# Q and K tiles with their heads' rows interleaved, each stored as 128 rows by one transfer

## The chip, the cores and the metric

The kernel runs on one core of a Trainium2 chip. A core has five engines with instruction streams of their own: TensorE (PE, the matmuls; PEld is its weight load), VectorE (DVE), ScalarE (ACT), GpSimd (POOL) and SyncE (SP). Here SP issues every DMA, in order. The transfers themselves run on the core's 16 DMA engines. Data lies in DRAM, in SBUF (128 partitions) or in PSUM (eight banks, which PE writes). The metric is the device time of one launch in microseconds: the median before is 1924.31 us over three runs (1919.36 to 1927.94).

## The reference, cut to what matters

Two layers over 2048 latent tokens of width 1024, with 256 context tokens. Layer 0 (even) runs windowed attention (8 query heads, 2 key/value heads of 64 dimensions, a sink for each head) beside a bidirectional S5 scan, both from one projection; layer 1 (odd) is a pooling mixer. The change touches the queries and keys of layer 0:

```python
q, k, v, g_attn, u, g_ssm = jnp.split(a @ w_in, cuts, axis=-1)
q = apply_axial_rope(q.reshape(b, l, ATTN_HEADS, HEAD_DIM), cos, sin)
k = apply_axial_rope(k.reshape(b, l, ATTN_KV_HEADS, HEAD_DIM), cos, sin)
...
s_loc = jnp.einsum('bnqhgd,bnkhd->bnhgqk', qb, kb).astype(jnp.float32) * scale
s_ctx = jnp.einsum('bnqhgd,bkhd->bnhgqk', qb, kc).astype(jnp.float32) * scale
p = jax.nn.softmax(jnp.concatenate([s_loc, s_ctx, s_sink], axis=-1), axis=-1)
out = (jnp.einsum('bnhgqk,bnkhd->bnqhgd', p_loc, vb)
       + jnp.einsum('bnhgqk,bkhd->bnqhgd', p_ctx, vc))
```

A score sums over the 64 dimensions of a head, so any order of these dimensions gives the same score if Q and K share it.

## The kernel before

Everything is fp32, and large products are made from parts: a value is split into a high part (float32r) and the rest (`split`, line 577), and a projection takes three matmuls for each block of 128 inputs (`products`, line 1020).

**The stages.** Up to about 90 us the kernel forms the adaptive-norm vectors and the statistics of the rows. Then come the projections: first those of u for the S5 scan, with K and V of the context (`t_u`), then `t_main` over two halves of the tokens. For each half it projects tiles of 128 columns by 512 tokens: m = 4 is K (both heads), m = 5 is V, m = 6 to 9 are Q (two heads each), m = 10 to 17 are gates. Between these matmuls stand those of S5: `t_s5u` loads u for a pair of channel groups from `u_scr` (line 1375), `t_s5e` tables from `e_scr`, `t_s5out` loads from `o_scr` and `r_scr` (lines 1529 and 1532) and stores the result to `z_scr` (line 1579). From about 690 us the attention runs in 32 units of one K/V head and 128 queries: `t_kv` loads and splits K and transposes V, `t_qk` loads Q and forms scores for four heads, DVE adds the mask and takes the maximum, ACT takes the exponential, POOL scales, PE transposes, and `t_pv` multiplies with V. The gates of the second half fill PE between. From about 1290 us on there is only layer 1, nearly all PE.

**A Q or K tile.** One PSUM bank holds a tile. Its 128 rows are [first rotation half of head A, the same of head B, second half of A, second half of B], 32 rows each, so the rotation is three products on DVE with cosine and sine (lines 1291 to 1293) and one sum on POOL (line 1297). The sum is stored to DRAM by two transfers (lines 1298 to 1300): rows 0 to 63 to the first 32 dimensions of two heads, rows 64 to 127 to the other 32. On the DRAM side such a transfer has the pattern [2 heads, 32 rows, 512 tokens]. K of the context goes the same way (line 1224).

**The loads.** `t_kv` needs K of one head twice, in partitions 0 to 63 and 64 to 127. It reads it by one transfer whose pattern begins with a step of zero taken twice, [0, 2], then 64 rows (line 1699); then it loads V (line 1700, 64 rows). Each job is loaded one job ahead of its use (line 1705). `t_qk` reads four heads by 128 queries into each half of the partitions, two transfers of 64 rows for each unit (lines 1765 to 1767), two units ahead.

**What sets the order.** The program's parts are generators, and a planner (`Threads`, lines 119 to 289) runs the one that is ready first by a model of costs; the order in which it runs them is the order of the instructions on each engine. For a DMA (`dma`, lines 220 to 239) the model keeps SP busy 0.55 us where either side has more than two dimensions, else 0.36 us for runs of 512 elements or more and 0.43 us for shorter ones; it holds a transfer back until the eighth one before it has landed (line 222), and it counts the data as spread over 16 engines, whatever the pattern. All DMAs are issued by line 513, all elementwise products and sums by line 465, activations by 499, matmuls by 505 and transposes by 509, so a line of the profile is told apart by its tiles: `x_r`, `core_r` and the like are regions of SBUF, `q_scr`, `k_scr`, `v_scr`, `u_scr`, `e_scr`, `o_scr`, `z_scr` and `sg_scr` (gates) are DRAM.

Of the kernel before, what the change touches and what calls it, by code (L numbers as in the profile page):

```python
# [15 lines left out]
T = 2048  # L16
D = 1024
CTX = 256
# [272 lines left out]
def body(ctx: ExitStack, tc: tile.TileContext, I, out):  # L291
# [34 lines left out]
        return drp.tile(list(shape), F32, name=name)  # L326

    a_scr = dram("a_scr", 2, KT, 128, 512)
    q_scr = dram("q_scr", 8, 64, T)
    k_scr = dram("k_scr", 2, 64, T + CTX)  # L330
    v_scr = dram("v_scr", 128, T + CTX)
    sg_scr = dram("sg_scr", 8, 128, T)
    u_scr = dram("u_scr", NG, L, 16, UCH)
# [845 lines left out]
    def t_u():  # L1179
        yield from wait("a4")  # L1180
        kv = yield from need(lambda: Ring(2, CTX))
        ub = {}
        for q in ORDER:
            yield from wait(f"a{q}")
            n = 512 if q < 4 else CTX
            tiles = range(6) if q == 4 else (0, 1, 2, 3) if q != ORDER[-1] else (2, 3, 0, 1)
            for m in tiles:
                yield from wait(f"wu{m}")
                if m < 4 and q in (4, ORDER[1]):
                    ub[q == 4, m] = yield from need(lambda: Buf(L, CCH if q == 4 else 64))  # L1190
                b = yield from gemm_bank()
                ps = bank(b, n)
                w = [shaped(wu[m].bufs[i].f, (KT, 128)) for i in range(2)]
                yield from products(ps, w, acts[q], last=m == tiles[-1] and q > 1)
                if tiles[0] == 2 and m == 3:
                    wu[2].free()
                    wu[3].free()
                k0, nk = (32 * (q % 2), 32) if q < 4 else (0, CCH)

                def evac(ps=ps, m=m, k0=k0, nk=nk, q=q, b=b):  # L1200
                    if m < 4:
                        o = ub[q == 4, m].f[:, ::-1, k0:k0 + nk].rearrange("p j k -> p k j")
                        act(o, ps.rearrange("p (k j) -> p k j", j=L), AF.Copy)
                        put_bank(b)
                        if q == 4 or q % 2 == 1:
                            def store():
                                src = ub[q == 4, m]
                                x0, nx = (0, CCH) if q == 4 else (CCH + 32 * (q - 1), 64)
                                for g in range(8):
                                    dma(u_scr[8 * m + g].rearrange("j c x -> c j x")[:, :, x0:x0 + nx],  # L1210
                                        src.f[16 * g:16 * g + 16])
                                if q in (4, ORDER[-1]):
                                    src.free()

                            todo.append(store)
                        return
                    o = kv.next()
                    act(o, ps, AF.Copy)
                    put_bank(b)

                    def store():
                        if m == 4:
                            for half in range(2):
                                dma(k_scr[:, 32 * half:32 * half + 32, T:], o[64 * half:64 * half + 64])
                        else:
                            dma(v_scr[:, T:], o)

                    todo.insert(0, store)

                todo.append(evac)  # L1230
            if q == 4:
                for r in wu[4:]:
                    r.free()
        for q in (0, 1):
            acts["b", q] = acts[q]
            flags.add(f"b{q}")
        yield from drain()
        for b in (kv, *wu[:2]):
            b.free()
        flags.add("u")  # L1240
# [9 lines left out]
    def t_main():  # L1250
        yield from t_u()
        yield from need(stage.fill)
        rope = yield from need(lambda: Ring(2, 2, 512))
        yield from wait("W0")
        W = s5.pop("W")
        yield from reopen("x1", X1, F32)
        flags.add("x1f")
        for h in range(2):
            tabs = []
            for c in range(2):  # L1260
                t_ = rope.next()
                dma(t_, I["rope"][:, :, 1024 * h + 512 * c:1024 * h + 512 * (c + 1)])
                tabs.append(t_)
            tiles = [(m + d, c) for m in range(4, 18, 2) for c in range(2) for d in range(2)]
            if h == 1:
                tiles = [x for x in tiles if x[0] < SOLO] + [(m, c) for c in range(2) for m in range(SOLO, 18)]
            for m, c in tiles:
                q = 2 * h + c
                yield from wait(f"b{q}")
                b = yield from gemm_bank()  # L1270
                ps = bank(b)
                j = 14 * h + m - 4
                alone = h == 1 and m >= SOLO
                if alone:
                    j += (18 - SOLO) * c
                if j == 10:
                    flags.add("again")
                if h == 1 and m == SOLO:
                    flags.add("kvqg_last")
                yield from products(ps, W.get(j, alone or c == 1), acts["b", q], last=m == 17)  # L1280

                def evac(ps=ps, m=m, t0=512 * q, tab=tabs[c], b=b):
                    if m == 5:
                        o = stage.next()
                        act(o, ps, AF.Copy)
                        put_bank(b)
                        todo.insert(0, lambda: dma(v_scr[:, t0:t0 + 512], o))
                    elif m < 10:
                        cos, sin = tab[:, 0], tab[:, 1]
                        t1, t2 = stage.next(), stage.next()  # L1290
                        tt(V, t1, ps, cos, OP.mult)
                        tt(V, t2[0:64], ps[64:128], sin[64:128], OP.mult)
                        tt(V, t2[64:128], ps[0:64], sin[0:64], OP.mult)
                        put_bank(b)

                        def more():
                            tt(G, t1, t1, t2, OP.add)
                            dst = k_scr if m == 4 else q_scr[2 * (m - 6):2 * (m - 6) + 2]
                            for half in range(2):
                                dma(dst[:, 32 * half:32 * half + 32, t0:t0 + 512], t1[64 * half:64 * half + 64])  # L1300
                            if (m, t0) == (9, 1536):
                                rope.free()

                        todo.insert(0, more)
                    else:
                        t1, t2 = stage.next(), stage.next()
                        act(t1, ps, AF.Tanh, scale=0.5)

                        def more():
                            stt(t2, t1, 1.0, ps, OP.add, OP.mult)  # L1310
                            put_bank(b)
                            todo.insert(0, lambda: dma(sg_scr[m - 10, :, t0:t0 + 512], t2))

                        todo.insert(0, more)

                todo.append(evac)
        W.free()
        flags.add("kvqg_w")
        yield from drain()
        flags.add("kvqg")  # L1320

        yield from t_out0()
        yield from t_l2()
        flags.add("end")
# [346 lines left out]
    def t_kv():  # L1671
# [12 lines left out]
        for s in range(8):  # L1684
            kv, n = UNITS[4 * s]
# [9 lines left out]
        def load(i):  # L1695
            if i < len(jobs):
                _, kv, _, _, t0, n, _ = jobs[i]
                r, v = raw.next()[:, :n], vt.next()[0:64, :n]
                dma(r, dap(k_scr, kv * 64 * (T + CTX) + t0, [0, 2], [T + CTX, 64], [1, n]))
                dma(v, v_scr[64 * kv:64 * kv + 64, t0:t0 + n])  # L1700
                got[i] = r, v

# [44 lines left out]
    def t_qk():  # L1747
# [13 lines left out]
        def load(u):  # L1761
            if u < NU:
                kv, n = UNITS[u]
                r = shaped(qraw.next(), (4, 128))
                for e in range(2):
                    dma(r[64 * e:64 * e + 64],
                        q_scr[4 * kv:4 * kv + 4, :, 128 * n:128 * n + 128].rearrange("h d t -> d h t"))
                qs[u] = r

        def prep(u):  # L1770
# [812 lines left out]
def _constants():  # L2583
# [30 lines left out]
    ang = np.stack([row[:, None] * inv, col[:, None] * inv], axis=1).reshape(T, 32).T  # L2614
    cos, sin = np.cos(ang).astype(f), np.sin(ang).astype(f)
    rope = np.zeros((128, 2, T), f)
    for b in range(4):
        rope[32 * b:32 * b + 32, 0] = cos
        rope[32 * b:32 * b + 32, 1] = sin if b < 2 else -sin
    return cst, rope  # L2620


def _layout(i):
# [26 lines left out]
    x1 = np.concatenate([np.arange(16), 32 + np.arange(16)])  # L2650
    x2 = x1 + 16
    order = [1280 + np.arange(512)]
    order.append(np.concatenate([512 + 64 * h + x for x in (x1, x2) for h in range(2)]))
    order.append(640 + np.arange(128))
    for p in range(4):
        order.append(np.concatenate([64 * h + x for x in (x1, x2) for h in (2 * p, 2 * p + 1)]))
    order.append(768 + np.arange(512))
    order.append(1792 + np.arange(512))
    order = np.concatenate(order)
# [47 lines left out]
```

## Time and profile before

| | |
|---|---|
| median of 3 runs | 1924.31 us |
| the profiled execution's own time | 1923.84 us |
| its span in the profile | 1921.9 us |
| mean granted TensorE clock | 0.957 |
| DMA packets, bytes | 241720, 286.16 MB |
| busy time of PE from 298 to 690 us | 367.68 of 392 us |
| busy time of PE from 690 to 1170 us | 384.04 of 480 us |

The page of a profile gives the busy time of each engine; the chain of waits goes back from the last instruction through whatever released each step, and gives start and length of each piece. A piece named DMA lasts from the issue to the landing. A piece named SPq is time of SP's queue. In a timeline the bracket after an instruction is the idle time of its engine before it, and what ended it. A row of windows gives, for each stretch, the busy time and the number of instructions of each engine, then the clock granted to TensorE, the mean busy share of the 16 DMA engines and what they moved.

### The profile page before, as it was taken

The page shows a single profiled execution, that of the slowest core. Times are in us where ns is not written, and L with a number is a line of the kernel's source. Part 1 is how long each engine was busy: PE and PEld are TensorE (multiplying, and loading weights), DVE is VectorE, ACT ScalarE, POOL GpSimd, SP SyncE. Part 2 cuts the span into 40 slices and gives each one's busy share as a digit, 9 for nine tenths or more (in the row PEclk, how much of TensorE's full clock was granted, in tenths as well). Part 3 has the DMA queues.
Part 4 walks back from the last instruction along what each step waited for, and adds up shares of the span by engine and source line. Part 5 has one row for each costly group of instructions (what it writes and reads, how often), then busy time and mean ns, then how long its engine had stood idle before and what let it go on. Part 6 is the DMA issues. An engine that isn't in the chain of part 4 may idle for free.

```text
span 1921.9 us, 24924 instructions
## 1 busy us (share of the span) xinstructions
PE 1753.0 (91%) x8488; PEld 1390.8 (72%) x8488; DVE 1284.6 (67%) x2182; ACT 827.9 (43%) x1689; POOL 549.2 (29%) x691
## 2 busy tenths in 40 slices
PE   7899998899998987878777898999899999999997
PEld 2554576678887865667666677888788888888897
DVE  4567869988886535576667875877555675566644
ACT  4545422355543424466665665644322243222321
POOL 4875653532433101242334542530000000000000
PEclk9999999999998987889898999999999999999999
DMA  8776483356654452444455563787411145351232
GB/s 294 211 251 198 130 251 117 113 158 201 191 184 128 127 171 69 109 122 124 134 160 154 151 183 93 221 266 230 129 53 55 44 154 185 115 153 61 87 94 86
DMA packets 241720, 286.16 MB, mean 149 GB/s; under 512 B 75832, under 2 KB 170808, under 8 KB 240568
## 3 DMA queue, kind: packets, MB, share of 16 engines
q1 hardware_dynamic: 241592, 284.56, 48.9%
q8 instruction: 67, 1.10, 0.2%
q14 instruction: 61, 0.50, 0.1%
HBM read 204.60 MB, written 79.89 MB: 148 GB/s over the span
## 4 chain that ended last, share of the span: by engine, by line
PE 68%; DVE 11%; DMA 8%; ACT 5%; issue 4%; POOL 3%; SPq 2%; DVEq 0%; ACTq 0%; POOLq 0%
PE psum L505 65%; PE psum L509 3%; DVE core_f L465 3%; DVE x_r L465 2%; ACT x_f L499 2%; SPq L513 2%; DVE x_f L484 2%; ACT x_r L499 1%; DMA x_f<-u_scr 1%; DVE core_f L476 1%; POOL core_f L465 1%; ACT core_f L499 1%; POOL core_f L470 1%; DVE core_r L465 1%; DMA o_scr<-core_f 1%
## 5 line engine op out<-in xcount | busy, mean ns | idle before, releaser
L505 PE MATMUL psum<-x_r,core_r 128*128 128x512 f32 (+3 forms) x4536 | 1104.1, 398 | 23.7 <-DVE x_r L465 11.0
L505 PEld LDWEIGHTS psum<-x_r,core_r 128*128 128x128 f32 x4536 | 850.2, 192 | 224.8 <-issue 22.3
L505 PE MATMUL psum<-x_r 128*128 128x256 f32 (+3 forms) x1808 | 378.9, 351 | 33.0 <-ACT core_f L499 16.1
L465 DVE TENSOR_TENSOR core_f<-core_f 128x512 f32<-128x512 f32 (+18 forms) x556 | 374.0, 694 | 49.6 <-ACT core_f L499 17.6
L505 PEld LDWEIGHTS psum<-x_r 128*128 128x128 f32 x1808 | 295.8, 198 | 76.1 <-ACT core_f L499 21.0
L465 DVE TENSOR_TENSOR core_r<-core_f,core_r 128x512 fp32r<-128x512 f32 (+1 forms) x172 | 127.7, 743 | 182.7 <-ACT core_r L499 182.6
L499 ACT ACTIVATE core_r<-core_f 128x512 fp32r<-128x512 f32 (+1 forms) x224 | 140.6, 631 | 245.2 <-PE psum L505 124.6
L465 POOL TENSOR_TENSOR core_f<-core_f 128x32 f32<-128x32 f32 (+5 forms) x257 | 164.8, 654 | 201.2 <-DVE core_f L465 61.6
L499 ACT ACTIVATE core_f<-psum 128x512 f32<-128x512 f32 (+2 forms) x217 | 115.4, 534 | 205.1 <-PE psum L505 158.2
L471 POOL TENSOR_SCALAR x_f<-x_f,core_f 128x640 f32<-128x640 f32 (+1 forms) x128 | 128.9, 1020 | 208.8 <-DVE core_f L493 164.2
L499 ACT ACTIVATE x_r<-core_f 128x512 fp32r<-128x512 f32 (+5 forms) x174 | 127.4, 744 | 110.4 <-DVE core_f L476 72.1
L484 DVE CUSTOM_DVE_ANT_0 x_f<-psum,x_f 128x640 f32<-128x640 f32 (+1 forms) x128 | 98.7, 771 | 113.3 <-PE psum L505 111.6
L499 ACT ACTIVATE x_f<-x_f,core_f 128x640 f32<-128x640 f32 (+2 forms) x154 | 122.7, 798 | 98.6 <-DVE core_f L476 94.8
L509 PE MATMUL psum<-core_f,x_f 128*128 128x128 f32 (+1 forms) x728 | 116.7, 285 | 25.0 <-DVE x_r L465 17.4
L499 ACT ACTIVATE core_f<-core_f 64x32 f32<-64x32 f32 (+8 forms) x225 | 84.1, 375 | 125.5 <-DVE core_f L476 100.5
L465 POOL TENSOR_TENSOR core_r<-core_f,core_r 128x512 fp32r<-128x512 f32 x52 | 77.3, 1489 | 204.7 <-ACT core_r L499 196.1
L476 DVE SCALAR_TENSOR_TENSOR core_f<-core_f 128x512 f32<-128x512 f32 (+13 forms) x162 | 118.2, 739 | 18.9 <-DMA core_f<-h_scr 11.6
L499 ACT ACTIVATE x_r<-psum 128x512 fp32r<-128x512 f32 (+2 forms) x174 | 96.5, 561 | 75.7 <-PE psum L505 59.5
L499 ACT ACTIVATE x_f<-psum 128x512 f32<-128x512 f32 (+5 forms) x187 | 77.5, 447 | 118.5 <-PE psum L505 104.2
L509 PEld LDWEIGHTS psum<-core_f,x_f 128*128 128x128 f32 (+1 forms) x728 | 90.9, 148 | 47.8 <-DVE x_r L465 24.0
L505 PE MATMUL psum<-x_f 128*128 128x128 f32 (+1 forms) x768 | 103.2, 287 | 16.9 <-DMA x_f<-u_scr 11.4
L465 DVE TENSOR_TENSOR x_r<-psum,x_r 128x512 fp32r<-128x512 f32 (+2 forms) x174 | 110.1, 646 | 10.6 <-ACT x_r L499 10.3
(63 smaller groups left out, 1212.1 us busy)
## 6 DMA issues: line engine op xcount, KB each, us to landing
core_f<-in_wo SPq DMA_DIRECT2D x48, 512.0 KB
core_f<-in_w SPq DMA_DIRECT2D x42, 512.0 KB
x_f<-in_adaM SPq DMA_DIRECT2D x32, 512.0 KB
core_f<-in_xT SPq DMA_DIRECT2D x46, 256.0 KB
x_f<-in_adaN SPq DMA_DIRECT2D x8, 1024.0 KB
o_scr<-core_f SPq DMA_DIRECT2D x32, 256.0 KB
x_f<-o_scr SPq DMA_DIRECT2D x16, 512.0 KB
sg_scr<-core_f SPq DMA_DIRECT2D x32, 256.0 KB
```

The source lines that it names most:

```text
L465: return e.tensor_tensor(o, a, b, op=op)
L470: return e.tensor_scalar(o, a, s1, None, op0=op0)
L471: return e.tensor_scalar(o, a, s1, s2, op0=op0, op1=op1)
L476: return V.scalar_tensor_tensor(o, a, s, b, op0=op0, op1=op1)
L484: return V.tensor_tensor_reduce(out=o, in0=a, in1=b, scale=scale, scalar=first, op0=op0, op1=op1, accum_out=accum)
L499: return S.activation(o, i, f, **kw)
L505: return TE.matmul(o, w, x, start=start, stop=stop)
L509: return TE.transpose(o, i, ident)
L513: return nc.sync.dma_start(o, i)
```

## The change

The columns of the weights are put in another order by the host, so that row 2d + e of a Q or K tile is dimension d (in rotated order) of head e of the pair; the first rotation half of both heads is still in rows 0 to 63. A Q tile now pairs heads h and h + 2 of the four that share a K/V head. The rope table is repeated to fit. In DRAM, `k_scr` has 128 rows in this order, and `q_scr` holds for each K/V head 128 rows with two tiles side by side. A tile is stored by one transfer of 128 rows. K of a head is every second row of `k_scr`, and its load becomes two transfers of 64 rows, one for each half of the partitions. The load of Q keeps its two transfers of 64 rows by four heads by 128 queries, with other steps: the four heads are now at steps of T elements behind each other.

```diff
-    q_scr = dram("q_scr", 8, 64, T)
-    k_scr = dram("k_scr", 2, 64, T + CTX)
+    q_scr = dram("q_scr", 2, 128, 2, T)
+    k_scr = dram("k_scr", 128, T + CTX)
...
                         if m == 4:
-                            for half in range(2):
-                                dma(k_scr[:, 32 * half:32 * half + 32, T:], o[64 * half:64 * half + 64])
+                            dma(k_scr[:, T:], o)
...
-                            dst = k_scr if m == 4 else q_scr[2 * (m - 6):2 * (m - 6) + 2]
-                            for half in range(2):
-                                dma(dst[:, 32 * half:32 * half + 32, t0:t0 + 512], t1[64 * half:64 * half + 64])
+                            dst = k_scr if m == 4 else q_scr[(m - 6) // 2, :, (m - 6) % 2]
+                            dma(dst[:, t0:t0 + 512], t1)
...
-                dma(r, dap(k_scr, kv * 64 * (T + CTX) + t0, [0, 2], [T + CTX, 64], [1, n]))
+                for e in range(2):
+                    dma(r[64 * e:64 * e + 64], dap(k_scr, kv * (T + CTX) + t0, [2 * (T + CTX), 64], [1, n]))
...
-                    dma(r[64 * e:64 * e + 64],
-                        q_scr[4 * kv:4 * kv + 4, :, 128 * n:128 * n + 128].rearrange("h d t -> d h t"))
+                    dma(r[64 * e:64 * e + 64], dap(q_scr, 256 * T * kv + 128 * n, [4 * T, 64], [T, 4], [1, 128]))
...
-    for b in range(4):
-        rope[32 * b:32 * b + 32, 0] = cos
-        rope[32 * b:32 * b + 32, 1] = sin if b < 2 else -sin
+    for b in range(2):
+        rope[64 * b:64 * b + 64, 0] = np.repeat(cos, 2, axis=0)
+        rope[64 * b:64 * b + 64, 1] = np.repeat(-sin if b else sin, 2, axis=0)
...
-    order.append(np.concatenate([512 + 64 * h + x for x in (x1, x2) for h in range(2)]))
+    order.append(np.concatenate([np.stack([512 + 64 * h + x for h in range(2)], 1).ravel() for x in (x1, x2)]))
...
-        order.append(np.concatenate([64 * h + x for x in (x1, x2) for h in (2 * p, 2 * p + 1)]))
+        h0 = 4 * (p // 2) + p % 2
+        order.append(np.concatenate([np.stack([64 * h + x for h in (h0, h0 + 2)], 1).ravel() for x in (x1, x2)]))
```

## The prediction, on record before the result

> **What bounds the kernel now.** I read the page's span and busy lines first, then the chain of waits, then PE's timeline at each place where the chain leaves PE for a transfer, then windows over those places.
>
> ```profile
> span 1921.9 us, 24924 instructions
> PE 1753.0 (91%) x8488; PEld 1390.8 (72%) x8488; DVE 1284.6 (67%) x2182; ACT 827.9 (43%) x1689; POOL 549.2 (29%) x691
> ```
>
> PE bounds the kernel: 168.9 us of the span are without a matmul, and only work taken out of those, or out of stretches at a lower clock, moves the end. Layer 2 (from 1380 us on one unbroken run of PE) holds nothing that the diff touches. So I look at the stores of Q and K (275 to 650 us) and at the start of the attention (about 690 us). The chain, start and length:
>
> ```profile
> 274.61 11.91 DMA k_scr<-core_f
> 286.54 4.59 DMA e_scr<-core_f
> ...
> 364.63 6.84 DMA x_f<-o_scr
> 371.49 7.77 DMA x_f<-u_scr
> ...
> 562.14 3.43 SPq L513
> 566.80 8.88 DMA z_scr<-x_f
> ...
> 597.10 9.03 DMA x_f<-u_scr
> 615.67 8.73 DMA x_f<-u_scr
> ...
> 688.28 10.21 DMA core_f<-v_scr
> 991.81 4.00 DMA core_f<-ss_scr
> 1012.23 3.97 DMA core_f<-att_scr
> 1380.10 529.40 PE psum L505 x2542
> ```
>
> A 256 KB load takes 4.0 us at 991 and 1012 us. A 128 KB store of K takes 11.91, loads of 288 KB (u_scr) 7.8 to 9.0, and a V load of at most 96 KB 10.21. Something holds these up that is gone later. Windows in which SP issues nothing new show it (columns: us, busy PE, PEld, DVE, ACT, POOL, then clock, DMA share, GB/s):
>
> ```profile
> core 0: us, PE busy (x) PEld busy (x) DVE busy (x) ACT busy (x) POOL busy (x), PEclk, DMA share, GB/s
> 609.00:612.00 3.00, 3.00 (x22) 2.73 (x22) 0.41 (x2) 0.97 (x4) 0.00 (x0) 0.96 0.13 51
> 650.00:653.00 3.00, 3.00 (x15) 2.49 (x14) 1.51 (x4) 2.85 (x6) 1.26 (x1) 1.00 0.13 51
> 697.00:698.00 1.00, 0.00 (x0) 0.00 (x0) 0.00 (x0) 0.00 (x0) 0.00 (x0) 0.50 0.14 53
> ```
>
> A share of 0.13 to 0.14 of sixteen DMA engines is two engines, at 51 GB/s together. The first two windows follow pairs of Q stores, the third K loads. What these have in common in the code is an access pattern on the DRAM side that begins with a dimension of two (`q_scr[2 heads, 32 rows, 512]`, `k_scr` with `[0, 2]`); the stores and loads beginning with 64 or 128 rows do not leave such a tail. So before, a Q or K tile of 256 KB sits on two engines for 262 KB / 51 GB/s = 5.1 us, and whatever is issued behind it is complete only when its own shares on those two engines are through. The V load is such a follower. (The Trainium skill, page "DMA: Bandwidth & Descriptors", section on why a DMA adds 16 to its semaphore, has the rule: the number of engines is the largest up to 16 that divides the slowest dimension of both sides; these windows agree with it, and by it the new patterns, which begin with 128 and 64, go on sixteen.) In the third window every engine of the core is idle.
>
> What PE loses to it, from its timeline (idle time in brackets):
>
> ```profile
> 292.45 0.90 PE L509 MATMUL psum<-core_f,x_f 128*128 128x128 f32 x3 [3.31 <-DVE x_f L465]
> 379.40 2.26 PE L505 MATMUL psum<-x_f 128*128 128x144 f32 x8 [4.85 <-DMA x_f<-u_scr]
> 579.97 2.26 PE L505 MATMUL psum<-x_f 128*128 128x144 f32 x8 [5.44 <-DVE x_f L476]
> 606.27 2.02 PE L505 MATMUL psum<-x_f 128*128 128x144 f32 x7 [3.41 <-DMA x_f<-u_scr]
> 624.45 1.25 PE L505 MATMUL psum<-x_f 128*128 128x144 f32 x8 [2.31 <-DMA x_f<-u_scr]
> 693.26 0.33 PE L509 MATMUL psum<-core_f 64*128 64x64 f32 x2 [3.10 <-DMA core_f<-v_scr]
> 698.53 0.58 PE L509 MATMUL psum<-core_f 64*128 64x64 f32 x3 [2.93 <-DMA core_f<-v_scr]
> ```
>
> These gaps sum to 25.35 us. After five of them the granted clock is at a half:
>
> ```profile
> 291.80:295.20 3.40, 2.75 (x9) 2.31 (x10) 3.31 (x7) 1.16 (x4) 0.33 (x1) 0.50 0.98 313
> 377.10:383.90 6.80, 4.50 (x14) 3.76 (x14) 5.49 (x10) 1.16 (x3) 1.75 (x2) 0.50 0.07 26
> 578.50:585.30 6.80, 5.33 (x18) 4.68 (x19) 1.32 (x2) 2.04 (x6) 2.53 (x2) 0.50 0.22 75
> 605.80:609.20 3.40, 2.93 (x11) 2.77 (x12) 3.37 (x7) 1.00 (x3) 1.27 (x1) 0.50 0.26 85
> 694.50:704.70 10.20, 7.27 (x19) 5.19 (x19) 2.84 (x7) 2.49 (x5) 0.00 (x0) 0.50 0.36 108
> ```
>
> PE works 2.75 + 4.50 + 5.33 + 2.93 + 7.27 = 22.8 us in them; at full clock that is half, so 11.4 us more. At most 36.8 us hang on the two-engine transfers.
>
> **The change, part by part.** *The order of columns* is made on the host, in the weights and the rope table; the matmuls, the products with cosine and sine and the shapes of the tiles are the same. Zero.
>
> *Q and K stores.* Each of 20 tiles (16 of Q, 4 of K) and the context K goes out by one transfer of 128 rows instead of two of 64.
>
> ```profile
> L513 SPq DMA_DIRECT2D q_scr<-core_f x32: 487/510/830, 298.1 to 641.2; - x32
> L513 SPq DMA_DIRECT2D core_f<-k_scr x18: 518/529/1214, 686.3 to 1058.0; - x18
> L513 SPq DMA_DIRECT2D sg_scr<-core_f x32: 314/380/1522, 375.0 to 823.8; - x32
> ```
>
> On SP a tile costs 2 x 0.51 us now and 0.38 after (the gate's store, same shape): 0.64 us less, 13 us over 20 tiles, beside PE's work; worth nothing by itself. What counts is landing: on sixteen engines I price the store, and the loads behind it, at the 4.0 us of the 256 KB rows. Place by place:
>
> 292.45: the last e store left SP 0.02 us after the K store had landed (274.61 + 11.91). The program keeps at most eight transfers open (the planner has the same rule, line 222), so SP stood. It could leave 2 us earlier and land in 4.0 instead of 4.59: 2.6 of 3.31, and 1.4 of clock: 4.0.
>
> 379.40: the u load left SP just as the o load landed (364.63 + 6.84). Both at 4.0: 6.6 us earlier. The whole 4.85 and 2.25: 7.1.
>
> 579.97: SP waited 3.43, then the z store took 8.88; at 4.0 that is over 8 us earlier. The whole 5.44 and 2.7: 8.1.
>
> 606.27 and 624.45: the u loads come 5.0 and 4.7 us earlier: 3.41 + 1.5 and 2.31: 7.2.
>
> *K loads.* Each of 18 becomes two of 64 rows, 0.53 us more on SP each time, 9.5 us in all. Behind them in SP's queue stand the V load of the same job, then the loads of weights and Q and the stores of the attention's output.
>
> ```profile
>   PE psum L509: 6.0, 2
>   ACT x_r L499: 8.3, 2
> ```
>
> These rows (who waited for the V loads, who for the K loads) say that only two jobs, the first two, are waited for; later ones are loaded a job ahead, so their extra issues cost nothing while that cover holds (0.53 us each where it does not). At 690 us the second V load leaves 1.1 us later but lands in 4.0 instead of 10.21: 5.1 of the 6.03 us, and 3.6 of clock: 8.7.
>
> Sum: 4.0 + 7.1 + 8.1 + 7.2 + 8.7 = 35.1. From this goes what is late next. In two of the gaps DVE worked without a break:
>
> ```profile
> 374.55:379.40 4.85, 0.00 (x1) 0.03 (x1) 4.82 (x6) 0.00 (x0) 4.30 (x3) 0.76 0.40 144
> 602.86:606.27 3.41, 0.00 (x1) 0.04 (x1) 3.38 (x5) 0.00 (x0) 1.28 (x1) 0.93 0.18 61
> 298.00:690.00 392.00, 367.68 (x1979) 304.88 (x1977) 316.23 (x498) 163.85 (x391) 135.33 (x103) 0.97 0.50 154
> 690.00:1170.00 480.00, 384.04 (x1971) 317.10 (x1971) 313.10 (x650) 275.03 (x596) 161.93 (x151) 0.89 0.48 133
> ```
>
> That is 8.2 us of work for which the gap made room. DVE has 76 us free in this stretch, so the loss lies between 0 and 8.2; I take all of it, since the stage's chain runs through DVE between the transfers. Gain 26.9 us.
>
> *The Q loads* read four runs of 512 B for each of 64 rows, as before. Zero, apart from no longer queueing behind K.
>
> *The planner.* The order of all instructions comes from a model that spreads every transfer over sixteen engines and charges SP 0.55 us for a transfer of more than two dimensions, 0.36 or 0.43 for others. In it SP loses 20 x 0.74 and gains 18 x 0.31 us, so some steps change places. The trace can't show it; I bound it by 10 us to either side, about one K or V wait at the attention's start with its clock, and take zero.
>
> **The rivals.** *DVE takes the gaps.* If DVE's order holds PE at every place between 298 and 690 us, only the first place (4.0) and the attention's start (8.7, where DVE too stands idle) are left: 1911. For it: DVE is busy 81% of the stretch. Against: PE is busy 94%, and the named releaser is a transfer at three gaps of four.
>
> *Halves serialize.* The Trainium skill, same page, "Rules for kernel authors", says that two transfers to disjoint halves of the partitions are not worth making, since they share the same engines; one of 128 is to be used. As a mechanism here: the pair of K loads would hold the V load as long as the single one did, so the last 8.7 us stay: 1905.5. Against: the old single load is the one that shows two engines' share, and the V load, of 64 rows, leaves no such tail.
>
> *A worse order in the attention.* PE idles 96 us in 480 there, 3.0 us for each of 32 units, as it waits in turn for DVE and ACT. If the new plan puts a unit's transposes or products ahead of what they wait for, such a unit loses another 3.0 and half of a 3.4 us clock window, 4.7 us. Six units eat the gain; from eight it is slower by over 0.5%: with ten, 1944. For it: the stage has little slack. Against: the edits move planned times by 1 us or less.
>
> *No change in kind.* The stores could stay on few engines for a reason that I don't see, the tail being set by the source rows: 1923.
>
> *More.* If DVE loses nothing and K's tails in the later attention also cost something: 1923.8 - 36.8 - 5 = 1882.
>
> **How the numbers follow.** The profiled execution took 1923.84 us, span 1921.9, against a median of 1924.31: the same, so the gain goes off either. Forecast: 1923.84 - 26.9 = 1897. Chances: forecast (1889 to 1905, the DVE term from zero to twice) 0.67; DVE takes the gaps 0.12; halves serialize 0.04; more 0.06; no change in kind, or gains lost to order, 0.05; worse order 0.06. The range goes from the case of more, 1882, to that of DVE with half of the planner's term, 1916; it leaves out the last two. A measurement of this kernel can tell about 0.5%, 9.6 us; all but the last two cases lie beyond that on the fast side, less 0.03 for DVE together with a poor order: faster 0.86, same 0.08, slower 0.06.
>
> **What would show it.** Right: 16 Q stores and 5 K stores at 0.4 us of SP, 36 K loads; no window at a share of 0.13 behind them; u loads on the chain under 6 us or none; PE's gaps at S5's u products, and the two before V's transposes, gone or under 1 us, with their half clock; PE's idle time from 298 us to the last S5 product down from 24 to under 15 us. Wrong: the tails gone and the same idle time with DVE or ACT as releaser (DVE takes the gaps); the tail still behind K loads (halves); more idle time per unit or more half-clock windows in the attention (order).

## The result, and the profile after

The changed kernel takes 1903.09 us (median of 4 runs, 1900.5 to 1906.46), against 1924.52 before: a ratio of 0.9892, 95% interval [0.9865, 0.9919]. It is faster by 21.4 us, in the direction forecast, 6 us slower than the 1897 predicted and inside the range. The profiled execution took 1902.7 us:

```profile
span 1900.9 us, 24927 instructions
PE 1746.3 (92%) x8488; PEld 1384.5 (73%) x8488; DVE 1286.8 (68%) x2183; ACT 827.8 (44%) x1689; POOL 550.2 (29%) x690
```

The other engines are as busy as before. What went is 14 us of PE's idle time (154.6 us of the span, 168.9 before) and 7 us of its busy time with the same 8488 matmuls; the mean granted clock rose from 0.957 to 0.965.

The stores and loads that the diff touches, by their tile (count, then shortest, median and longest time on SP's queue in ns, then first and last start):

```profile
L513 SPq DMA_DIRECT2D x_f<-q_scr x64: 512/562/4077, 667.8 to 1143.6; - x64
L513 SPq DMA_DIRECT2D q_scr<-core_f x16: 319/334/403, 294.8 to 618.1; - x16
...
```

```profile
L513 SPq DMA_DIRECT2D core_f<-k_scr x36: 444/594/1482, 662.3 to 1015.8; - x36
L513 SPq DMA_DIRECT2D k_scr<-core_f x5: 320/393/531, 91.1 to 548.5; - x5
```

The last Q store starts 23.1 us earlier than before (641.2), the first Q load 23.9 us earlier (691.7).

The traces also hold each transfer's increments of its semaphore (the counter that tells when it has landed), which these views leave out. Before, each of the 60 Q and K stores and K loads has three: one within 1.7 us of the issue, two at the landing. The u load that SP issued at 597.10 us, behind two Q stores, has sixteen: fourteen after 2.42 to 3.40 us, the last two after 7.72 and 9.03. The V load of 688.28 us, behind two K loads, has fourteen after 3.74 to 4.25 us and two after 9.23 and 10.21. Read as one increment for each engine that lands its share, a Q or K tile lies on two engines, and a transfer behind it waits for its own two shares there, the others long done. Between 270 and 1170 us 97 transfers show such a late pair (the fifteenth over 1 us behind the fourteenth, the sixteenth over 2 us). In the changed kernel every Q and K transfer has sixteen, and in that stretch no late pair is left.

Up to 717 us (752 before) PE takes its matmuls in the same order in both kernels, so the seven that waited in the prediction's list can be found again, in the new timeline of PE:

```profile
291.01 0.60 PE L509 MATMUL psum<-core_f,x_f 128*128 128x128 f32 x4
...
372.36 1.15 PE L505 MATMUL psum<-x_f 128*128 128x144 f32 x8
...
567.24 1.15 PE L505 MATMUL psum<-x_f 128*128 128x144 f32 x8
...
587.77 1.15 PE L505 MATMUL psum<-x_f 128*128 128x144 f32 x8
...
601.99 1.15 PE L505 MATMUL psum<-x_f 128*128 128x144 f32 x8
...
667.52 0.33 PE L509 MATMUL psum<-core_f 64*128 64x64 f32 x2
669.37 0.39 PE L509 MATMUL psum<-core_f 64*128 64x64 f32 x3
```

None of them has idle time before it any more, and the half clock after them is gone up to the attention: from 513 to 680 us the trace grants the full clock throughout. From the first Q store to the first Q load (first row) PE idles 11.1 us of 373.0 (before, in the stretch from 298 to 690 us, 24.3 of 392); the second row, from 589 to 607 us, holds the u products that waited 2.31 us at 624.45 before, and PE has no gap in it:

```profile
294.80:667.80 373.00, 361.92 (x1984) 300.36 (x1982) 326.69 (x501) 165.59 (x393) 139.40 (x103) 0.99 0.53 163
...
589.00:607.00 18.00, 18.00 (x111) 16.04 (x110) 14.94 (x24) 8.10 (x21) 5.31 (x4) 1.00 0.46 146
```

So at the attention's start the gain is larger than at the end. The stores of the attention's output, before and after, one row each, give the first and the last of its units:

```profile
L513 SPq DMA_DIRECT2D att_scr<-core_f x64: 580/607/1618, 766.8 to 1258.3; - x64
```

```profile
L513 SPq DMA_DIRECT2D att_scr<-core_f x64: 580/608/1348, 732.4 to 1235.5; - x64
```

The first unit ends 34.4 us earlier, the last 22.8: from the first unit's store to the last one's the attention takes 503.1 us instead of 491.5 and gives back 11.6 us. The experiments ask whether this is the transfers' doing or the planner's order.

### The profile page after: what moved, and what is told of

Its sections match the earlier page's. It is cut to its first block, busy times and chain, and to the rows that moved or that the text cites. A ratio compares the mean times of both kernels' runs of the same rounds, so it can differ in the third digit from the quotient of the medians.

```text
span 1900.9 us, 24927 instructions
## 1 busy us (share of the span) xinstructions
PE 1746.3 (92%) x8488; PEld 1384.5 (73%) x8488; DVE 1286.8 (68%) x2183; ACT 827.8 (44%) x1689; POOL 550.2 (29%) x690
## 4 chain that ended last, share of the span: by engine, by line
PE 70%; DVE 15%; ACT 5%; DMA 5%; issue 4%; SPq 1%; POOL 1%; DVEq 0%; ACTq 0%; POOLq 0%
PE psum L505 67%; DVE core_f L465 5%; DVE x_r L465 3%; PE psum L509 3%; ACT x_f L499 2%; DVE x_f L484 2%; ACT x_r L499 1%; DVE core_f L476 1%; DVE x_f L465 1%; ACT core_f L499 1%; SPq L513 1%; DMA core_f<-sg_scr 1%; DVE core_r L465 1%; DVE x_r L476 0%; DMA h_scr<-core_f 0%
## 5 line engine op out<-in xcount | busy, mean ns | idle before, releaser
L505 PE MATMUL psum<-x_r,core_r 128*128 128x512 f32 (+3 forms) x4536 | 1100.5, 397 | 32.7 <-DVE core_f L476 17.3
L505 PEld LDWEIGHTS psum<-x_r 128*128 128x128 f32 x1808 | 296.9, 199 | 72.0 <-ACT core_f L499 13.2
L465 DVE TENSOR_TENSOR core_r<-core_f,core_r 128x512 fp32r<-128x512 f32 (+1 forms) x168 | 121.6, 725 | 172.5 <-ACT core_r L499 172.4
L471 POOL TENSOR_SCALAR x_f<-x_f,core_f 128x640 f32<-128x640 f32 (+1 forms) x128 | 123.8, 979 | 207.6 <-DVE core_f L493 156.1
L465 POOL TENSOR_TENSOR core_r<-core_f,core_r 128x512 fp32r<-128x512 f32 x56 | 84.3, 1509 | 213.6 <-ACT core_r L499 202.8
L509 PE MATMUL psum<-core_f,x_f 128*128 128x128 f32 (+1 forms) x728 | 118.5, 288 | 26.8 <-DVE x_r L465 22.8
L480 POOL COPY core_f<-core_f 128x16 f32<-128x16 f32 (+2 forms) x35 | 9.7, 289 | 373.6 <-DVE core_f L476 293.2
```

The source lines that it names most:

```text
L465: return e.tensor_tensor(o, a, b, op=op)
L471: return e.tensor_scalar(o, a, s1, s2, op0=op0, op1=op1)
L480: return e.tensor_copy(o, a)
L505: return TE.matmul(o, w, x, start=start, stop=stop)
L509: return TE.transpose(o, i, ident)
```

## The experiments

My theory: the gain up to the attention's start comes from the transfers' landing earlier, because they run on more engines; what the attention gives back comes from the new order alone. The rivals: the extra K transfers or the new steps of the Q loads slow the attention; or two half transfers serialize; or it is their number that counts.

To hold the order, the planner's book-keeping is separated from the transfer: `plan` charges the model alone, `nc.sync.dma_start` issues the transfer alone. Fed with the old patterns, the planner puts the instructions of PE, DVE, ACT and POOL where they stood before; in the traces their sequences are the same. ("Order" includes a choice of engine: the planner also decides whether DVE or POOL makes the low part of a split, and one such group has 172 instructions on DVE before and 168 in the changed kernel.)

**The whole change in the old order.**

```diff
-                            dma(dst[:, t0:t0 + 512], t1)
+                            w = T + CTX if m == 4 else T
+                            plan(*((dap(dst.tensor, 32 * x * w + t0, [64 * w, 2], [w, 32], [1, 512]),
+                                    t1[64 * x:64 * x + 64]) for x in range(2)))
+                            nc.sync.dma_start(dst[:, t0:t0 + 512], t1)
...
-                    dma(r[64 * e:64 * e + 64], dap(k_scr, kv * (T + CTX) + t0, [2 * (T + CTX), 64], [1, n]))
+                    nc.sync.dma_start(r[64 * e:64 * e + 64], dap(k_scr, kv * (T + CTX) + t0, [2 * (T + CTX), 64], [1, n]))
```

(Ahead of the loop, `plan` charges the old K load once; the context K is treated as the tiles are.)

> The whole change, but the planner is fed the costs of the transfers before, so that every engine's instructions stand in the order of before. Theory (the gain up to the attention's start is earlier landing, and what the attention gives back is the planner's new order): the 33 us that the changed kernel has gained by 715 us stay, and the attention gives nothing back: 1886 to 1892. Rival (the extra K transfers or the new steps of the Q loads slow the attention, whatever the order): about 1903, as the changed kernel.

Measured: 1891.19 us, ratio 0.9841 [0.9825, 0.9856]; 12 us faster than the changed kernel by the medians, 10 by the two ratios (the changed kernel's interval begins at 0.9865), with the very same transfers.

```profile
L513 SPq DMA_DIRECT2D att_scr<-core_f x64: 586/610/1437, 734.9 to 1225.4; - x64
```

First unit 31.9 us earlier than before, last 32.9. The attention takes 490.5 us, as before (491.5). The 18 extra K loads (36 of about 0.59 us on SP instead of 18 of 0.53, some 11 us more in all) and the new steps of the Q loads cost it nothing; both parts of that rival are out.

**The new order with the old transfers**, the reverse: the kernel before, its model fed with the new patterns.

```diff
-                            for half in range(2):
-                                dma(dst[:, 32 * half:32 * half + 32, t0:t0 + 512], t1[64 * half:64 * half + 64])
+                            plan(dap(dst.tensor, t0, [T, 128], [1, 512]), t1)
+                            for half in range(2):
+                                nc.sync.dma_start(dst[:, 32 * half:32 * half + 32, t0:t0 + 512], t1[64 * half:64 * half + 64])
```

(The context K and the K load are planned by the new patterns in the same way.)

> The transfers and the layout of before, but the planner is fed the costs of the changed transfers, so that every engine's instructions stand in the changed kernel's order. Theory (the new order costs the attention 10 to 16 us): 1932 to 1942. Rival (the order is harmless): 1920 to 1928.

Measured: 1935.82 us, ratio 1.0073 [1.005, 1.0095]: 13.2 us slower than before.

```profile
L513 SPq DMA_DIRECT2D att_scr<-core_f x64: 580/605/1707, 766.3 to 1271.4; - x64
```

The first unit is where it was (766.3), the last 13.1 us later: all of the loss lies in the attention (505.1 us). The stretch from the eighth to the 24th unit, in the kernel before, then here, then in the changed kernel:

```profile
895.00:1145.50 250.50, 206.64 (x1103) 170.39 (x1101) 187.64 (x364) 160.64 (x342) 106.91 (x95) 0.91 0.56 155
```

```profile
888.80:1157.60 268.80, 216.40 (x1116) 178.54 (x1117) 184.60 (x366) 161.52 (x344) 103.33 (x93) 0.89 0.53 147
```

```profile
854.60:1123.70 269.10, 216.09 (x1118) 179.09 (x1118) 183.62 (x367) 161.66 (x344) 104.33 (x93) 0.90 0.54 147
```

With the old transfers it is 18.3 us longer than before, with 13 more matmuls of 1103; from the first to the eighth unit 5.7 us had been won (122.5 instead of 128.2). PE idles 52.4 us instead of 43.9, and is busy 9.8 us longer at a lower mean clock (0.89, 0.91). The changed kernel shows the same: 269.1 us, with 53.0 of idle time. Who PE waits for there, before and here:

```profile
PE psum L509 <- DVE x_r L465: 16.4, 13, 3.6
...
PE psum L505 <- DVE core_f L476: 1.3, 1, 1.3
```

```profile
PE psum L509 <- DVE x_r L465: 19.9, 15, 3.5
...
PE psum L505 <- DVE core_f L476: 6.5, 3, 3.2
```

The transposes wait 3.5 us longer for the low parts of the split, and three products wait for a DVE step (line 476) where one did; the waits for line 499 on ACT, not shown, come to 17.3 us instead of 18.3. That the order costs this is shown; which swap of steps does it is not, since the two orders differ in hundreds of places.

**The stores alone**, stores and planning as in the first experiment, K loaded by one transfer that still begins with a dimension of two:

```diff
-                for e in range(2):
-                    dma(r[64 * e:64 * e + 64], dap(k_scr, kv * (T + CTX) + t0, [2 * (T + CTX), 64], [1, n]))
+                dma(r, dap(k_scr, kv * (T + CTX) + t0, [0, 2], [2 * (T + CTX), 64], [1, n]))
```

> Order of before, stores by one transfer of 128 rows, but K loaded by one transfer that begins with the dimension of two. Theory: the gaps between 290 and 625 us go (24 to 26 us), those two before V's transposes at the attention's start stay (6 us and a half clock after them): 1897 to 1901. Rival (extra K transfers cost the attention): here they are absent, so 1890 or less.

Measured: 1897.42 us, ratio 0.988 [0.9863, 0.9898]: 25.3 us of gain. The waits for V stay:

```profile
667.17 0.33 PE L509 MATMUL psum<-core_f 64*128 64x64 f32 x2 [1.18 <-DMA core_f<-v_scr]
673.00 0.58 PE L509 MATMUL psum<-core_f 64*128 64x64 f32 x3 [3.91 <-DMA core_f<-v_scr]
...
```

and in the second of these gaps two engines' share is back, 0.15 at 50 GB/s:

```profile
671.00:672.50 1.50, 0.00 (x0) 0.00 (x0) 0.07 (x1) 0.52 (x1) 0.00 (x0) 0.75 0.15 50
```

**The K load alone**: kernel, layout, stores and order of before.

```diff
-                dma(r, dap(k_scr, kv * 64 * (T + CTX) + t0, [0, 2], [T + CTX, 64], [1, n]))
+                th.dma(r, src, False)
+                for e in range(2):
+                    nc.sync.dma_start(r[64 * e:64 * e + 64], k_scr[kv, :, t0:t0 + n])
```

(`src` is the old pattern.)

> The kernel before with its order, layout and stores; only the K load is two transfers of 64 rows. Theory: the V loads at 690 us land in about 4 us, the two gaps of 3 us and their half clock go: 1914 to 1917. Rival (two halves take the same engines and serialize): 1922 to 1926. Rival (18 more issues on SP cost the attention 0.5 us each): 1924 to 1933.

Measured: 1911.2 us, ratio 0.9935 [0.9914, 0.9956]: 11.5 us of gain; the time is 2.8 us below the range expected, and why is not shown. The six runs lie apart, four from 1911.1 to 1913.7 us and two at 1902.8 and 1903.7, and the profiled one is the latter; its lines tell where waits are gone, not how much the median gains. Both rivals are out, since 1911 lies below 1922 and 1924: the two halves do not hold up the V load, and the first V transposes go without a wait, while the u products still wait for the stores, as before:

```profile
608.02 2.26 PE L505 MATMUL psum<-x_f 128*128 128x144 f32 x8 [3.31 <-DMA x_f<-u_scr]
...
691.83 0.33 PE L509 MATMUL psum<-core_f 64*128 64x64 f32 x2
693.69 0.39 PE L509 MATMUL psum<-core_f 64*128 64x64 f32 x3
```

25.3 and 11.5 make 36.8, both together 31.5; the difference is within what the intervals of the three ratios leave open.

**Stores by halves, each spread over the engines**: against the first experiment's kernel, rows 0 to 63 and 64 to 127 are stored apart in the new layout, both patterns beginning with 64.

```diff
-                            nc.sync.dma_start(dst[:, t0:t0 + 512], t1)
+                            for x in range(2):
+                                nc.sync.dma_start(dst[64 * x:64 * x + 64, t0:t0 + 512], t1[64 * x:64 * x + 64])
```

> Order of before and the new layout, but each Q and K tile is stored by two transfers of 64 rows, each on its own spread over the engines, instead of one of 128. Theory (what counted was the number of engines that a transfer runs on, not the number of transfers): 1889 to 1894, as with one transfer. Rival (fewer transfers, and with them SP's time and the eight open places, made the gain): 1900 to 1915.

Measured: 1892.24 us, ratio 0.9848 [0.9824, 0.9871], the same as with one transfer (0.9841). So "stored by one transfer" is not what pays; that the pattern no longer begins with two is. For the K load this stands apart from the layout: the kernel before, with its layout, gained by the load's pattern alone. For the stores, layout and pattern changed together in every run; that the layout alone does nothing is not shown, but in all of these traces that were counted (before, after, and the first five experiments) a transfer of Q or K has two increments at the landing where its pattern begins with two, and sixteen where it doesn't. (The Trainium skill, page "DMA: Bandwidth & Descriptors", section "Rules for kernel authors", calls two transfers to disjoint halves of the partitions not worth making against one of 128. As a statement on the same rows this run agrees, 1892.2 and 1891.2 us; against the old K load, which began with two, the halves gained 11.5 us.)

**Three more orders**, all with the changed kernel's transfers. First the planner is fed the old K load:

> The changed kernel, but the planner is fed the cost of the old K load, so its order comes from the new stores alone. Theory (the 13 us are the price of one particular order, drawn by the new costs): anywhere from 1886 to 1908, with the difference to 1891 falling between the attention's units. Rival (the two-part K load in the model is what spoils the order): 1891 or less, and the other half, stores planned as before, about 1904.

Then the old stores:

> The changed kernel, but the planner is fed the cost of the old stores, so its order comes from the new K load alone. Theory (a particular order is drawn): anywhere from 1886 to 1908. Rival (the K load's cost in the model spoils the order): about 1904.

Then nothing old, but `DMAF = 1.12` in place of 1.1:

> The changed kernel with one constant of the planner moved by 2% (DMAF from 1.1 to 1.12), which alone gives another order. Theory (the order's price is a draw that any small change of the model's costs makes anew): differs from 1903 by up to 20 us to either side, nearly all of it between the attention's units. Rival (only the change's own costs move the order's price): 1900 to 1906.

Measured: 1894.86 [0.9843, 0.9896], 1896.97 [0.9848, 0.992] and 1902.41 us [0.9876, 0.9925]. With 1891.2 and 1903.1 these are five orders of the same transfers within 12 us; the intervals of the first two overlap both ends. The rivals for the first two are not borne out: neither cost alone spoils the order by 12 us in the median. The stores of the attention's output, in the same sequence:

```profile
L513 SPq DMA_DIRECT2D att_scr<-core_f x64: 580/608/2191, 731.5 to 1234.4; - x64
```

```profile
L513 SPq DMA_DIRECT2D att_scr<-core_f x64: 586/611/1599, 733.6 to 1233.8; - x64
```

```profile
L513 SPq DMA_DIRECT2D att_scr<-core_f x64: 586/612/1931, 747.7 to 1238.1; - x64
```

In the first two the attention takes 502.9 and 500.2 us, so what they lose lies between the units, as the theory said (the first one's profiled run, 1901.1 us, is the slowest of its four). For the third the theory was wrong on the place: its first unit ends 15.3 us later than the changed kernel's (732.4), and its attention takes 490.4 us. Its time lies in the rival's range, 1900 to 1906, as well as in the theory's; only the place tells that this order is another one. (Half of its Q loads also go to another region of SBUF, so it is not the order alone that differs.)

The version to keep is the whole change in the old order, 1891.2 us: faster than both kernels.

## Why the prediction was right, and where it was not

**The cause** was right: Q and K transfers on two engines, and everything behind them late. Stores alone give 25.3 us and K loads alone 11.5, against 26.4 and 8.7 in the sum, and the number of transfers, held apart from the spread, makes no difference that the intervals show.

**The sum of places** before the DVE term was 35.1 us, and it holds, place by place. The start of the same matmul in the two traces gives the gain as it grows. The changed kernel's trace is 2.0 us behind at 30 us already, ahead of every Q or K transfer, and still at 288 us; then the first place gives 4.1 (4.0 forecast), 379 us 5.1 (7.1), 580 us 7.8 (8.1), 606 and 624 us together 7.7 (7.2), the attention's start 9.4 (8.7): 34 in all.

**"I take all of it", the 8.2 us for DVE**, was too much, and right in kind at one place. At 379 us the gain was 7.1 at first, as forecast, and fell back by 2.3 in three waits that were 0.62 us in all before:

```profile
389.16 2.05 PE L505 MATMUL psum<-x_f 128*128 128x128 f32 x16 [0.71 <-DVE core_f L476]
...
392.52 1.12 PE L505 MATMUL psum<-core_f 128*48 128x272 f32 x4 [0.87 <-ACT x_f L499]
...
399.25 3.02 PE L505 MATMUL psum<-x_r,core_r 128*128 128x512 f32 x12 [1.19 <-DVE core_f L476]
```

At the other place, 606 us, nothing was lost. So about 2 us of the 8.2 came true. That DVE worked without a break in two gaps showed that it had work ready, not that PE would have to wait for all of it: DVE is busy 326.69 of 373.0 us in this stretch, 88% instead of 81%, and PE still idles only 11.1 us.

**"I bound it by 10 us to either side ... and take zero", the planner's term**, failed in size: the order alone costs 13.2 us (9.6 to 18.3 by the interval), with the new transfers 12 by the medians and 10 by the ratios. It is the largest error, and the DVE term hid part of it: 35.1 less 11.6 would have been 23.5 of gain, and 21.4 were measured. That the time came within 6 us of the forecast is in part luck, since some 6 us too much for DVE stood against 10 to 13 too little for the order. The rival of a worse order had the right mechanism and place, PE waiting longer between the units and more half clock, and took it for unlikely because planned times move by 1 us or less. Small moves of planned times are no bound for the cost of an order: a 2% change of one constant makes another order that is 11 us slower than the old one, by a loss in another place.

**The price of 4.0 us for a landing** did not hold everywhere. The chain after still holds one K store:

```profile
276.29 8.39 DMA k_scr<-core_f
284.70 4.51 DMA e_scr<-core_f
...
547.16 3.13 DMA x_f<-u_scr
```

This one is issued behind ten loads for S5 that SP issued in the 6.3 us before; from 276.3 to 284.7 us the sixteen DMA engines are busy for a share of 0.94, so it waited behind these loads on all of them, as far as the trace tells; no run tests it. The u load at 547 us, with little ahead of it, lands in 3.13. The forecast did not suffer: the e store left SP at 284.70 instead of 286.54 and PE had no gap behind it.

## What to carry to other kernels

Look at how each DRAM pattern begins: a transfer whose outer dimension is two shows up as a share of 0.13 of sixteen engines, and its price is paid by whatever is issued behind it. It is found by a landing far longer than that of other transfers of the size, then by the share in a window in which SP issues nothing, and most surely by the increments: fourteen early and two late. Where a planner makes the order, a change is worth trying with the order held as well: here that told 31.5 us of gain from the 10 to 13 us that an order cost.

## What the runs showed of the hardware that was not expected

Two transfers of 64 rows each cost the same as one of 128 (1892.2 and 1891.2 us), though the Q stores then take 17.1 us of SP's queue instead of 5.4. And the K load, moved by two transfers instead of one from the same rows, took 36 issues of 0.59 us instead of 18 of 0.53, and was still worth 11.5 us by itself.
